# Norms, transposes and operand splits rank 80 earlier in the order of work, and a half's modulation is divided evenly between VectorE and ScalarE

## The chip, the core and the metric

The kernel runs on one core of a Trainium2 chip. The metric is the device time of one execution in microseconds (us). Inputs and outputs are f32 in HBM; nothing of the input is reordered on the way in beyond packed weight arrays, which the kernel streams in their order of use.

The engines, by the names of the profile: PE is TensorE (matmuls and transposes; PEld its weight loads), DVE is VectorE, ACT is ScalarE, POOL is GpSimd, SP is SyncE, which here only issues transfers (DMA).

## The reference

Two models run one after the other on 256 tokens of width 1024, with f32 accuracy. The first has two layers: layer 0 mixes with sliding-window attention and a gated delta rule, layer 1 with a gated recurrence, and each is followed by a squared-ReLU MLP of width 4096. The second has two layers over two streams, the tokens and a context of 256; its mixer joins latent attention (MLA), a 31-tap convolution and a short convolution, and is followed by the same kind of MLP. Cut to what matters:

```python
# first model, both layers
x = layer_norm(DN_ALPHA * x + mix, ln1_g[layer], ln1_b[layer])
x = layer_norm(DN_ALPHA * x + sqrelu_mlp(x, mlp_w1[layer], mlp_w2[layer]), ln2_g[layer], ln2_b[layer])

# second model
def modulation(cvec, w_mod, b_mod):
    m = jax.nn.silu(cvec) @ w_mod + b_mod
    return jnp.split(m[:, None, :], N_MOD, axis=-1)

def modulate(h, shift, scale):
    return h * (1.0 + scale) + shift

def rmsnorm(u, g):
    y = u * lax.rsqrt(jnp.mean(u * u, axis=-1, keepdims=True) + EPS)
    return y * g
```

Each layer of the second model takes `modulate(rmsnorm(x))` into its mixer and into its MLP, and adds `gate * rmsnorm(output)` back to `x`. A layer's six modulation rows come from a matrix of 1024 x 6144.

## The kernel before

**Tiling.** Tokens lie on the 128 partitions: `xt0` and `xt1` are the two token tiles of the main stream, `xc0` and `xc1` those of the context, 128 x 1024 each. A matmul with weights needs its activations transposed, channels on partitions, and to keep f32 accuracy every operand is split in two f32r parts: a high part, the cast of the value, and a low part, value minus high part. A product is three matmuls, high by high, high by low and low by high (`wh`, `wl` are the weights' parts; tiles named `b` hold activations' parts). Weights come in units of 128 x 2048 (`wr`, two buffers) and are split by halves of 1024 (`w_split`, L393 to L409): ScalarE casts the high part (L407), VectorE subtracts for the low part (L408), four buffers each.

**The steps that the change touches.** `to_xT` (L628) turns a token tile's half (512 channels) into operands: four transposes on TensorE into one PSUM bank (`pb` for the first half, `pc` for the second; L366), and then one of two ends. Without modulation, `split` (L454, L455): ScalarE casts, VectorE subtracts. With modulation, 28 halves of the second model: four chunks of 128 x 128 get scale and shift, three on VectorE (L645), one on ScalarE (L647), into one tile `y`; ScalarE casts `y` to the high part (L648), VectorE subtracts (L649). `ln_post` (L654) is the layer norm of the first model. `normed` (L1398) is the second model's norm before a modulation: two sums of squares on ScalarE (L1389), one small VectorE instruction (L1394), the power -1/2 on GpSimd (L1395) and two VectorE scalings (L1408). `post_norm` (L1411) runs `add_normed`: the same sums, two VectorE products with the gate row (L1421, L1423), GpSimd's power (L1395) and two VectorE instructions that add to the stream (L1426).

**What sets the order.** The code is written once, in a straight line, and a scheduler orders each engine's instructions by a rank that counts up as the code is read. `tc.high_priority(n)` sets the rank back by n for what is written under it, so it comes n places earlier than the code says, as far as dependences and buffers allow. Engines run their lists strictly in order: an instruction that waits holds back all behind it. Before the change `post_norm` has 5; the layer-norm chain, `normed` and `to_xT` have none; weight splits have `WS.ahead`; matmuls that fill (`pm`, below) have -10.

**Filling.** The modulation rows are computed by 384 matmuls into tiles `pm` (weights `wm`, `mods()`), which are sprinkled between the others wherever the code calls `fill`.

**Buffers.** Tiles are named by pool: `s2` and `s4` are scratch tiles of 512 and 1024, `ti` the tiny ones, `row` the broadcast rows (3 buffers), `pa` the PSUM banks in which products are summed.

Of the kernel before, what the change touches and what calls it, by code (L numbers as in the profile page):

```python
# [15 lines left out]
P = 128  # L16
BIG = 1.0e30
SM = 1.0 / math.sqrt(96.0)
NW = 4
LEAD = 96  # L20
TRAIL = 24
ALPHA = 4.0 ** 0.25
# [271 lines left out]
def hybrid_then_mla(ctx: ExitStack, tc: tile.TileContext, a, out, usizes):  # L294
# [22 lines left out]
    def s2(shape, dt=F32):  # L317
        return tmp.tile(shape, dt, tag="s2", bufs=9, name=nm("s2"))
# [25 lines left out]
    def v3(ap, n):  # L344
        return ap.rearrange("p (a b) -> p a b", a=n)
# [19 lines left out]
    def tr(o, i):  # L365
        T.transpose(o, i, ident)  # L366
# [86 lines left out]
    def split(ps, h, l):  # L453
        S.copy(h, ps)  # L454
        V.tensor_tensor(l, ps, f(h), op=SUB)  # L455
# [172 lines left out]
    def to_xT(src, t, xT, hfs=(0, 1), off=0, bank=None, mod=None):  # L628


        for hf in hfs:
            ps = (bank or (psB, psC)[hf])()
            for c in range(4):
                o = 512 * hf + 128 * c - off
                tr(ps[:, 128 * c : 128 * c + 128], src[:, o : o + 128])
            sl = (slice(None), slice(4 * hf, 4 * hf + 4), slice(128 * t, 128 * t + 128))
            if mod is None:
                split(v3(ps, 4), xT[0][sl], xT[1][sl])
                continue
            i, st, kind = mod  # L640
            y = s2([P, 4, 128])
            for c in range(4):
                A, B = mcol(i, st, kind, hf, c), mcol(i, st, kind - 1, hf, c)
                if c < 3:
                    V.tensor_scalar(y[:, c, :], ps[:, 128 * c : 128 * c + 128], A, B, op0=MUL, op1=ADD)  # L645
                else:
                    S.activation(y[:, c, :], ps[:, 128 * c : 128 * c + 128], AF.Identity, bias=B, scale=A)  # L647
            S.copy(xT[0][sl], y)  # L648
            V.tensor_tensor(xT[1][sl], y, f(xT[0][sl]), op=SUB)  # L649

    def new_xT():
        return (b8([P, 8, 256], F32R), b8([P, 8, 256], F32R))

    def ln_post(t, halves, g, b, late):  # L654

        x = xt[t]
        st = ti(12, "st", 4)
        for c in range(2):
            cs = slice(512 * c, 512 * c + 512)
            V.scalar_tensor_tensor(x[:, cs], x[:, cs], ALPHA, halves[c], op0=MUL, op1=ADD)  # L660
            V.bn_stats(st[:, 6 * c : 6 * c + 6], x[:, cs])
        mv = ti(2)
        V.bn_aggr(mv, st)
        rs = ti(1)
        rsqrt(rs, mv[:, 1:2], 1, 1.0, 1e-5)
        both = slice(0, 512), slice(512, 1024)
        for cs in both:
            V.scalar_tensor_tensor(x[:, cs], x[:, cs], mv[:, 0:1], g[:, cs], op0=SUB, op1=MUL)
        for cs in both:
            V.scalar_tensor_tensor(x[:, cs], x[:, cs], rs, b[:, cs], op0=MUL, op1=ADD)  # L670
        if late is not None:
            late.fn[t] = lambda: to_xT(x, t, late.xT)

    def softplus(o, x, n):

# [68 lines left out]
    def mcol(i, st, kind, hf, c):  # L744

        o = 8 * c + 4 * (kind % 2) + 2 * hf + (1 - st)
        return mc[:, i, kind // 2, o : o + 1]
# [649 lines left out]

    def normed(x):  # L1398

        ss = ti(2)  # L1400
        y = s4([P, 1024])
        for c in range(2):
            cs = slice(512 * c, 512 * c + 512)
            sumsq(ss[:, c : c + 1], x[:, cs], y[:, cs], 1.0 / 32.0)
        r = rms(ss)
        for c in range(2):
            cs = slice(512 * c, 512 * c + 512)
            V.tensor_scalar(y[:, cs], x[:, cs], r, None, op0=MUL)  # L1408
        return y

    def post_norm(x, halves, GP):  # L1411

        with tc.high_priority(5):
            add_normed(x, halves, GP)

    def add_normed(x, halves, GP):
# [650 lines left out]
```

## Time and profile before

| | |
|---|---|
| median of 3 runs | 1632.86 us (1632.76 to 1634.14) |
| the profiled execution | 1635.88 us, of which the span is 1633.8 us and 2.1 us lie around it |
| PE busy | 1578.0 us, 97% of the span |
| DVE busy | 1029.0 us, 63% |
| ACT busy | 743.3 us, 45% |
| POOL busy | 94.8 us, 6% |
| mean granted clock of TensorE | 0.991 of full speed |

How to read it: PE is busy nearly all the time, so the time that can be had or lost lies in its idle stretches, about 56 us in all, and in stretches in which its clock is at half speed. The view of waits of an engine says what ended its idle time, the timeline shows single instructions with their start, duration and the idle time before them, and the table of stretches gives each engine's busy time and the granted clock between two times. Times on a timeline are us from the start of the span. An instruction's duration can be longer than its distance to the next one on the same engine, because one's end overlaps the next one's start.

### The profile page before, as it was taken

What the parts mean: (1) busy time and instruction counts of PE and PEld (TensorE: products, weight loads), DVE (VectorE), ACT (ScalarE), POOL (GpSimd) and SP (SyncE); (2) the same over time, 40 slices, a digit from 0 to 9 for tenths busy, and PEclk for the clock granted to TensorE, in tenths of its full rate; (3) what the DMA queues carried; (4) which work ended last, traced back from release to release, by engine and by line L of the source; (5) the groups of instructions that cost most, each with busy time, mean ns of one, the idle gap of its engine ahead of it and who ended that gap; (6) DMA issues with size and microseconds to landing.
All of it is one profiled execution on the core that took longest, in us unless ns stands there. A gap on an engine that the chain in (4) does not pass through costs nothing.

```text
span 1633.8 us, 24905 instructions
## 1 busy us (share of the span) xinstructions
PE 1578.0 (97%) x10182; PEld 1358.9 (83%) x10182; DVE 1029.0 (63%) x1593; ACT 743.3 (45%) x1264; POOL 94.8 (6%) x121
## 2 busy tenths in 40 slices
PE   7999999999999999999999999999999999989998
PEld 7866679888878998877877789999999788779997
DVE  6874575556787556768974753444444789775555
ACT  5642244443574445436454543222222475554443
POOL 0021000000000000003010100000000030000000
PEclk9999999999999999999999999999999999989999
DMA  7865475555665554562310432222232262235553
GB/s 289 288 217 172 167 258 196 204 207 191 248 258 181 194 192 169 181 227 80 130 52 27 138 134 89 93 103 85 97 104 79 100 216 107 73 126 201 181 186 124
DMA packets 46946, 259.77 MB, mean 159 GB/s; under 512 B 5600, under 2 KB 5856, under 8 KB 24304
## 3 DMA queue, kind: packets, MB, share of 16 engines
q1 hardware_dynamic: 46832, 258.18, 44.9%
q8 instruction: 80, 1.31, 0.3%
q14 instruction: 34, 0.28, 0.1%
HBM read 257.08 MB, written 1.08 MB: 158 GB/s over the span
## 4 chain that ended last, share of the span: by engine, by line
PE 78%; DVE 8%; ACT 4%; DMA 2%; POOL 1%; issue 1%; POOLq 0%; DVEq 0%; ACTq 0%; SPq 0%
PE pa L342 44%; PE pb L342 27%; PE pm L342 4%; PE pb L366 2%; DVE wl L408 1%; DMA wr<-in_wp_dram 1%; PE pc L366 1%; ACT s L1389 1%; ACT wh L407 1%; DVE s L1583 1%; POOL ti L1395 1%; ACT s L1652 0%; DVE s L645 0%; DVE b L711 0%; DVE xt L1426 0%
## 5 line engine op out<-in xcount | busy, mean ns | idle before, releaser
L408 DVE TENSOR_TENSOR wl<-wr,wh 128x1024 fp32r<-128x1024 f32 (+2 forms) x366 | 443.4, 1217 | 301.4 <-ACT wh L407 288.4
L407 ACT CAST wh<-wr 128x1024 fp32r<-128x1024 f32 (+2 forms) x364 | 376.1, 1041 | 405.8 <-PE pa L342 202.6
L342 PE MATMUL pa<-wh,b 128*128 128x512 f32 (+3 forms) x1456 | 411.1, 365 | 12.5 <-ACT b L816 5.7
L342 PE MATMUL pb<-b,wh 128*128 128x256 f32 x2240 | 406.2, 284 | 0.0
L342 PEld LDWEIGHTS pb<-b,wh 128*128 128x128 f32 x2240 | 352.7, 192 | 7.2 <-issue 3.4
L342 PE MATMUL pb<-b,wl 128*128 128x256 f32 x1120 | 317.8, 284 | 0.0
L342 PEld LDWEIGHTS pa<-wh,b 128*128 128x128 f32 x1456 | 267.6, 195 | 57.1 <-ACT b L648 6.1
L342 PE MATMUL pa<-wl,b 128*128 128x512 f32 (+3 forms) x728 | 258.7, 364 | 8.9 <-DVE wl L408 8.9
L342 PE MATMUL pa<-wh,s 128*128 128x512 f32 x768 | 244.5, 391 | 0.0
L342 PEld LDWEIGHTS pb<-b,wl 128*128 128x128 f32 x1120 | 215.1, 192 | 1.7 <-issue 1.7
L342 PE MATMUL pa<-b,wh 128*128 128x256 f32 x1056 | 199.2, 289 | 3.7 <-ACT wh L407 1.9
L342 PEld LDWEIGHTS pa<-b,wh 128*128 128x128 f32 x1056 | 166.2, 193 | 16.0 <-issue 4.4
L342 PEld LDWEIGHTS pa<-wl,b 128*128 128x128 f32 x728 | 142.3, 195 | 35.3 <-DVE wl L408 13.5
L342 PEld LDWEIGHTS pa<-wh,s 128*128 128x128 f32 x768 | 144.4, 188 | 28.9
L342 PE MATMUL pa<-b,wl 128*128 128x256 f32 x528 | 150.1, 288 | 1.3 <-DVE wl L408 1.3
L342 PE MATMUL pa<-wl,s 128*128 128x512 f32 x384 | 150.4, 392 | 0.0
L342 PEld LDWEIGHTS pa<-b,wl 128*128 128x128 f32 x528 | 101.6, 193 | 8.2 <-DVE wl L408 3.3
L560 DVE TENSOR_TENSOR s<-s 128x512 f32<-128x512 f32 x80 | 54.9, 687 | 50.2 <-ACT s L558 50.2
L342 PE MATMUL pm<-wm,cs_t 128*32 128x512 f32 x384 | 83.2, 606 | 1.9 <-DMA wm<-in_wm_dram 1.7
L342 PEld LDWEIGHTS pa<-wl,s 128*128 128x128 f32 x384 | 72.3, 188 | 14.5 <-DVE wl L408 1.2
L1583 DVE SCALAR_TENSOR_TENSOR s<-cu,cols_sb,s 128x512 f32<-128x512 f32 (+1 forms) x120 | 70.7, 621 | 0.5
L366 PE MATMUL pb<-kc_sb,s 128*128 128x128 f32 x366 | 56.8, 279 | 10.8 <-DVE s L1408 2.5
(278 smaller groups left out, 1391.6 us busy)
## 6 DMA issues: line engine op xcount, KB each, us to landing
wr<-in_wp_dram SPq DMA_DIRECT2D x176, 1024.0 KB, 4.8
wm<-in_wm_dram SPq DMA_DIRECT2D x96, 512.0 KB, 5.2
row<-in_rows_dram SPq DMA_DIRECT2D x10, 512.0 KB, 5.5
wr<-in_wp_dram SPq DMA_DIRECT2D x4, 832.0 KB
s<-in_bg_dram SPq DMA_DIRECT2D x24, 128.0 KB, 5.6
row<-mdr SPq DMA_DIRECT2D x6, 512.0 KB, 3.5
wr<-in_wp_dram SPq DMA_DIRECT2D x4, 264.0 KB, 3.6
b<-in_xT_dram SPq DMA_DIRECT2D x4, 256.0 KB, 6.1
```

What stands on the lines that cost most here:

```text
L342: T.matmul(o, l, r, start=start, stop=stop)
L366: T.transpose(o, i, ident)
L407: S.copy(h[:, :n], r)
L408: V.tensor_tensor(l[:, :n], r, f(h[:, :n]), op=SUB)
L560: V.tensor_tensor(q, r, r, op=MUL)
L1389: S.activation(j, x, AF.Square, scale=scale, accum_out=o)
L1395: G.tensor_tensor(r, e, half[:, :1], op=POW)
L1583: V.scalar_tensor_tensor(ac, src, w(k), ac, op0=MUL, op1=ADD)
```

## The change

`to_xT`, the layer-norm chain (now a function `ln_chain`), `normed` (its body now `rms_normed`) and `post_norm` run under `tc.high_priority(CHAIN)` with `CHAIN = 80`; `post_norm` had 5. In a modulated half the chunks 0 and 1 are VectorE's and 2 and 3 ScalarE's, where VectorE had three; and the high part is cast by VectorE (`V.tensor_copy`) and not by ScalarE.

```diff
+CHAIN = 80
@@ def to_xT(src, t, xT, hfs=(0, 1), off=0, bank=None, mod=None):
-        for hf in hfs:
...
-            for c in range(4):
-                A, B = mcol(i, st, kind, hf, c), mcol(i, st, kind - 1, hf, c)
-                if c < 3:
...
-            S.copy(xT[0][sl], y)
-            V.tensor_tensor(xT[1][sl], y, f(xT[0][sl]), op=SUB)
+        with tc.high_priority(CHAIN):
+            for hf in hfs:
+                ps = (bank or (psB, psC)[hf])()
+                for c in range(4):
+                    o = 512 * hf + 128 * c - off
+                    tr(ps[:, 128 * c : 128 * c + 128], src[:, o : o + 128])
+                sl = (slice(None), slice(4 * hf, 4 * hf + 4), slice(128 * t, 128 * t + 128))
+                if mod is None:
+                    split(v3(ps, 4), xT[0][sl], xT[1][sl])
+                    continue
+                i, st, kind = mod
+                y = s2([P, 4, 128])
+                for c in range(4):
+                    A, B = mcol(i, st, kind, hf, c), mcol(i, st, kind - 1, hf, c)
+                    if c < 2:
+                        V.tensor_scalar(y[:, c, :], ps[:, 128 * c : 128 * c + 128], A, B, op0=MUL, op1=ADD)
+                    else:
+                        S.activation(y[:, c, :], ps[:, 128 * c : 128 * c + 128], AF.Identity, bias=B, scale=A)
+                V.tensor_copy(xT[0][sl], y)
+                V.tensor_tensor(xT[1][sl], y, f(xT[0][sl]), op=SUB)
@@ def ln_post(t, halves, g, b, late):
-        x = xt[t]
+        with tc.high_priority(CHAIN):
+            ln_chain(xt[t], halves, g, b)
+        if late is not None:
+            late.fn[t] = lambda: to_xT(xt[t], t, late.xT)
+
+    def ln_chain(x, halves, g, b):
@@ def normed(x):
+        with tc.high_priority(CHAIN):
+            return rms_normed(x)
+
+    def rms_normed(x):
@@ def post_norm(x, halves, GP):
-        with tc.high_priority(5):
+        with tc.high_priority(CHAIN):
```

The counts of instructions stay the same on every engine but for the 28 halves: ScalarE has 28 casts fewer and 28 chunks more, VectorE 28 chunks fewer and 28 casts more. GpSimd's order stays the same. Of SP's transfers, three weight units (`wr96`, `wr102`, `wr110`) are issued two to five places later and two pairs of `wm` earlier.

The lines of the kernel after are numbered a few higher: L408 is L409, L645 is L647, the cast (L648 before) is L650, L649 is L651, L1394 is L1399, L1408 is L1417, L1421, L1423 and L1426 are L1430, L1432 and L1435.

The first place is TensorE around the second layer's MLP input, at 1433 to 1441 us of the trace before. `pa_1512` is the last bank of the mixer's output product for a token tile, `pb_1523` and `pc_1525` are the transposes of the normed tile `xt0`, `pa_1540` the head of the next product. Before:

```order
L342 MATMUL pa_1512_13426<-wl300_13502,b8_1471_13267 128x512
L342 MATMUL pa_1512_13426<-wh300_13501,b8_1472_13268 128x512
L342 MATMUL pa_1512_13426<-wh301_13507,b8_1471_13267 128x512
L342 MATMUL pa_1512_13426<-wl301_13508,b8_1471_13267 128x512
L342 MATMUL pa_1512_13426<-wh301_13507,b8_1472_13268 128x512
L366 MATMUL pb_1523_13587<-kc_sb_76,s4_1520_13554 128x128 x4
L366 MATMUL pc_1525_13599<-kc_sb_76,s4_1520_13554 128x128 x4
L342 MATMUL pa_1540_13659<-wh302_13511,b8_1507_13421 128x256
```

After:

```order
L343 MATMUL pa_1512_13426<-wl300_13502,b8_1471_13267 128x512
L367 MATMUL pb_1523_13587<-kc_sb_76,s4_1520_13554 128x128 x4
L367 MATMUL pc_1525_13599<-kc_sb_76,s4_1520_13554 128x128 x4
L343 MATMUL pa_1512_13426<-wh300_13501,b8_1472_13268 128x512
L343 MATMUL pa_1512_13426<-wh301_13507,b8_1471_13267 128x512
L343 MATMUL pa_1512_13426<-wl301_13508,b8_1471_13267 128x512
L343 MATMUL pa_1512_13426<-wh301_13507,b8_1472_13268 128x512
L343 MATMUL pa_1540_13659<-wh302_13511,b8_1507_13421 128x256
```

The eight transposes stand ahead of the last four matmuls of `pa_1512` and not behind them.

The second is VectorE at the same place, 1434 to 1442 us. `wl302` to `wl305` are low parts of weights, `s2_1524` and `s2_1526` the two modulated halves of `xt0`, `b8_1507` and `b8_1508` their high and low parts; `s2_1528`, `s2_1529` and `ti_1531` belong to the post-norm of the other token tile, `xt1`. Before:

```order
L408 TENSOR_TENSOR wl302_13512<-wr152_13505,wh302_13511 128x1024
L408 TENSOR_TENSOR wl303_13640<-wr152_13505,wh303_13639 128x1024
L645 TENSOR_SCALAR s2_1524_13592<-pb_1523_13587,mc_96 128x128 x3
L645 TENSOR_SCALAR s2_1526_13604<-pc_1525_13599,mc_96 128x128 x3
L1421 TENSOR_TENSOR s2_1528_13612<-pa_1511_13425,row_1506_13419 128x512
L1394 SCALAR_TENSOR_TENSOR ti_1531_13618<-ti_1527_13611 128x1
L1423 TENSOR_TENSOR s2_1529_13613<-pa_1512_13426,row_1506_13419 128x512
L649 TENSOR_TENSOR b8_1508_13422<-s2_1524_13592,b8_1507_13421 128x4x128
L649 TENSOR_TENSOR b8_1508_13422<-s2_1526_13604,b8_1507_13421 128x4x128
L1426 SCALAR_TENSOR_TENSOR xt1_90<-s2_1528_13612,ti_1532_13619,xt1_90 128x512
L1426 SCALAR_TENSOR_TENSOR xt1_90<-s2_1529_13613,ti_1532_13619,xt1_90 128x512
```

After:

```order
L409 TENSOR_TENSOR wl302_13512<-wr152_13505,wh302_13511 128x1024
L647 TENSOR_SCALAR s2_1524_13592<-pb_1523_13587,mc_96 128x128 x2
L647 TENSOR_SCALAR s2_1526_13604<-pc_1525_13599,mc_96 128x128 x2
L409 TENSOR_TENSOR wl303_13640<-wr152_13505,wh303_13639 128x1024
L1430 TENSOR_TENSOR s2_1528_13612<-pa_1511_13425,row_1506_13419 128x512
L1399 SCALAR_TENSOR_TENSOR ti_1531_13618<-ti_1527_13611 128x1
L1432 TENSOR_TENSOR s2_1529_13613<-pa_1512_13426,row_1506_13419 128x512
L1435 SCALAR_TENSOR_TENSOR xt1_90<-s2_1528_13612,ti_1532_13619,xt1_90 128x512
L1435 SCALAR_TENSOR_TENSOR xt1_90<-s2_1529_13613,ti_1532_13619,xt1_90 128x512
L650 CAST b8_1507_13421<-s2_1524_13592 128x4x128
L650 CAST b8_1507_13421<-s2_1526_13604 128x4x128
L651 TENSOR_TENSOR b8_1508_13422<-s2_1524_13592,b8_1507_13421 128x4x128
```

The whole post-norm of `xt1` stands ahead of the two casts that make the high parts of `xt0`, and `wl303` behind the modulation's chunks.

The third is VectorE in the first layer, at 921 to 930 us, where a context tile's post-norm (`xc0`), the modulation of `xt1` (`s2_1016`, `s2_1018`) and two weight splits meet. Before:

```order
L408 TENSOR_TENSOR wl213_8598<-wr107_8591,wh213_8597 128x1024
L645 TENSOR_SCALAR s2_1016_8785<-pb_1015_8780,mc_96 128x128 x3
L645 TENSOR_SCALAR s2_1018_8797<-pc_1017_8792,mc_96 128x128 x3
L1421 TENSOR_TENSOR s2_1020_8805<-s4_958_8419,row_982_8607 128x512
L1394 SCALAR_TENSOR_TENSOR ti_1023_8811<-ti_1019_8804 128x1
L1423 TENSOR_TENSOR s2_1021_8806<-s4_958_8419,row_982_8607 128x512
L649 TENSOR_TENSOR b8_978_8602<-s2_1016_8785,b8_977_8601 128x4x128
L1426 SCALAR_TENSOR_TENSOR xc0_4721<-s2_1020_8805,ti_1024_8812,xc0_4721 128x512
L649 TENSOR_TENSOR b8_978_8602<-s2_1018_8797,b8_977_8601 128x4x128
L1426 SCALAR_TENSOR_TENSOR xc0_4721<-s2_1021_8806,ti_1024_8812,xc0_4721 128x512
L408 TENSOR_TENSOR wl214_8930<-wr107_8591,wh214_8929 128x1024
```

After:

```order
L647 TENSOR_SCALAR s2_1016_8785<-pb_1015_8780,mc_96 128x128 x2
L647 TENSOR_SCALAR s2_1018_8797<-pc_1017_8792,mc_96 128x128
L1430 TENSOR_TENSOR s2_1020_8805<-s4_958_8419,row_982_8607 128x512
L1432 TENSOR_TENSOR s2_1021_8806<-s4_958_8419,row_982_8607 128x512
L647 TENSOR_SCALAR s2_1018_8797<-pc_1017_8792,mc_96 128x128
L409 TENSOR_TENSOR wl213_8598<-wr107_8591,wh213_8597 128x1024
L1399 SCALAR_TENSOR_TENSOR ti_1023_8811<-ti_1019_8804 128x1
L650 CAST b8_977_8601<-s2_1016_8785 128x4x128
L1435 SCALAR_TENSOR_TENSOR xc0_4721<-s2_1020_8805,ti_1024_8812,xc0_4721 128x512
L1435 SCALAR_TENSOR_TENSOR xc0_4721<-s2_1021_8806,ti_1024_8812,xc0_4721 128x512
L651 TENSOR_TENSOR b8_978_8602<-s2_1016_8785,b8_977_8601 128x4x128
L650 CAST b8_977_8601<-s2_1018_8797 128x4x128
```

`wl214` follows next. Ahead of it stand four chunks of the modulation where there were six, one low part where there were two, and two casts.

## Rows read from the trace of the kernel before

**Rows 1.** The page: busy time of PE, its share, instructions.

```profile
PE 1578.0 (97%) x10182; PEld 1358.9 (83%) x10182; DVE 1029.0 (63%) x1593; ACT 743.3 (45%) x1264; POOL 94.8 (6%) x121
```

**Rows 2.** Waits of PE: line, releaser and its line; us total, times, longest.

```profile
PE pa L342 <- DVE wl L408: 10.2, 8, 2.4
PE pa L342 <- ACT b L648: 7.0, 4, 4.1
...
PE pb L366 <- DVE s L1408: 2.5, 3, 1.1
...
PE pc L366 <- ACT s L647: 2.1, 2, 1.9
PE pc L366 <- DVE s L1725: 2.0, 4, 1.2
...
PE pa L342 <- ACT b L454: 0.8, 2, 0.6
```

**Rows 3.** Groups by line and shape: count, busy us, mean ns; idle before, releaser.

```profile
L648 ACT CAST b<-s 128x512 fp32r<-128x512 f32 x28 | 17.3, 618 | 0.5
L645 DVE TENSOR_SCALAR s<-pb,mc 128x128 f32<-128x128 f32 x42 | 15.0, 404 | 7.0 <-PE pb L366 7.0
...
L1408 DVE TENSOR_SCALAR s<-xt,ti 128x512 f32<-128x512 f32 x16 | 7.1, 484 | 4.2 <-POOL ti L1395 4.1
...
L647 ACT ACTIVATE s<-pb,mc 128x128 f32<-128x128 f32 x14 | 6.4, 456 | 18.5 <-DVE s L645 18.4
...
L405 DVE CAST wh<-wr 128x1024 fp32r<-128x1024 f32 x2 | 1.4, 688 | 0.0
```

**Rows 4.** Stretches: from:to, length, busy of PE, PEld, DVE, ACT, POOL; clock, DMA.

```profile
690.00:780.00 90.00, 84.18 (x550) 69.13 (x548) 68.47 (x126) 47.89 (x97) 17.06 (x24) 0.98 0.41 148
...
1280.00:1345.00 65.00, 60.24 (x388) 50.47 (x387) 56.18 (x124) 40.85 (x92) 15.21 (x25) 1.00 0.44 148
```

**Rows 5.** PE timeline, 205 to 208 us and 753: start, duration, line, instruction.

```profile
205.56 1.05 PE L342 MATMUL pm<-wm,cs_t 128*32 128x512 f32 x2
206.53 0.39 PE L342 MATMUL pa<-wh,b 128*128 128x256 f32 x1
206.85 1.05 PE L342 MATMUL pm<-wm,cs_t 128*32 128x512 f32 x4
207.83 0.38 PE L342 MATMUL pa<-wl,b 128*128 128x256 f32 x1
...
752.93 1.92 PE L342 MATMUL pm<-wm,cs_t 128*32 128x512 f32 x2
```

**Rows 6.** DVE timeline, 921 to 931 us: the split of `wl214`.

```profile
928.82 1.22 DVE L408 TENSOR_TENSOR wl<-wr,wh 128x1024 fp32r<-128x1024 f32 x1
```

**Rows 7.** PE timeline, two heads: idle time and its releaser in brackets.

```profile
930.09 0.58 PE L342 MATMUL pa<-wl,b 128*128 128x256 f32 x1 [2.22 <-DVE wl L408]
...
1439.28 0.58 PE L342 MATMUL pa<-wh,b 128*128 128x256 f32 x1 [4.14 <-ACT b L648]
```

**Rows 8.** DVE timeline, 1434 to 1442 us.

```profile
1434.28 2.35 DVE L408 TENSOR_TENSOR wl<-wr,wh 128x1024 fp32r<-128x1024 f32 x2
1436.54 1.04 DVE L645 TENSOR_SCALAR s<-pb,mc 128x128 f32<-128x128 f32 x3
...
1439.72 1.28 DVE L649 TENSOR_TENSOR b<-s,b 128x512 fp32r<-128x512 f32 x2
1440.92 0.75 DVE L1426 SCALAR_TENSOR_TENSOR xt<-s,ti,xt 128x512 f32<-128x512 f32 x1
```

**Rows 9.** PE by stretches of 3.4 us: length, busy; granted clock, DMA share, GB/s.

```profile
1438.40:1441.80 3.40, 2.52 (x12) 0.50 0.63 265
...
929.80:933.20 3.40, 3.11 (x14) 0.50 0.59 188
```

**Rows 10.** POOL timeline: start, duration of the power of a norm.

```profile
646.38 0.55 POOL L1395 TENSOR_TENSOR ti<-ti,half 128x1 f32<-128x1 f32 x1 [135.36 <-DVE ti L1394]
...
930.25 1.40 POOL L1395 TENSOR_TENSOR ti<-ti,half 128x1 f32<-128x1 f32 x1 [3.47 <-DVE ti L1394]
```

More of the change, by code (lines that the diff above doesn't have):

```diff
@@ L628, in to_xT @@
     def to_xT(src, t, xT, hfs=(0, 1), off=0, bank=None, mod=None):
-        for hf in hfs:
-            ps = (bank or (psB, psC)[hf])()
-            for c in range(4):
[L634 to L642, printed above, removed]
-                A, B = mcol(i, st, kind, hf, c), mcol(i, st, kind - 1, hf, c)
-                if c < 3:
-                    V.tensor_scalar(y[:, c, :], ps[:, 128 * c : 128 * c + 128], A, B, op0=MUL, op1=ADD)
-                else:
-                    S.activation(y[:, c, :], ps[:, 128 * c : 128 * c + 128], AF.Identity, bias=B, scale=A)
-            S.copy(xT[0][sl], y)
-            V.tensor_tensor(xT[1][sl], y, f(xT[0][sl]), op=SUB)
+        with tc.high_priority(CHAIN):
[18 more added lines that the diff above has]
+                V.tensor_tensor(xT[1][sl], y, f(xT[0][sl]), op=SUB)
     def new_xT():
@@ L670, in ln_post @@
             V.scalar_tensor_tensor(x[:, cs], x[:, cs], rs, b[:, cs], op0=MUL, op1=ADD)
-        if late is not None:
-            late.fn[t] = lambda: to_xT(x, t, late.xT)
     def softplus(o, x, n):
```

## The prediction

> **What bounds the kernel now.** I read the page first. PE is busy for 97% of the span [rows 1], so whatever DVE and ACT save counts only where PE stands idle, some 56 us. The view of PE's waits comes next, since it tells who ends that idle time. Few of its entries touch the change: heads of products that wait for the high part of a modulated half, 7.0 us in four waits, the longest 4.1; transposes that wait for `normed`'s scalings, 2.5, for ScalarE's chunk of a modulation, 2.1 (a buffer: `pc` can't be written until its last reader is done), and for the branch norms, 2.0; and a plain operand split, 0.8 [rows 2]. That makes 14.4 us at most. The largest entry, 10.2 us for weights' low parts, belongs to no raised step [rows 2]; DVE's own list decides there. Last I read the granted clock by stretches: after long waits PE runs a stretch of 3.4 us at half speed, 0.50 at 1438.4 and 929.8 [rows 9]. In such a stretch half of the work of 3.4 us is lost, 1.7 us. So a wait has a second price, and one that is shortened may give back more than itself.
>
> **The modulation itself.** Before, a half's path behind its transposes is three DVE chunks, one ACT chunk, the ACT cast. A DVE chunk alone takes 0.40, and three take 1.04, so one more adds 0.32 [rows 3, 8]; the ACT chunk 0.46, the cast 0.62 [rows 3]. Sum 1.04 + 0.46 + 0.62 = 2.1. After: two DVE chunks 0.72, two ACT chunks 0.46 + about 0.40, then a DVE cast. The trace has no DVE cast of 512 elements. The nearest are a DVE cast of 1024 at 0.69, half of which is 0.34, and a DVE scaling of 512 from SBUF at 0.48 [rows 3]; a subtraction of that size at 0.64, two in 1.28 [rows 8], is the upper bound, since it reads a second tensor. I take 0.42, between the first two. The path is then 2.0: a gain of 0.1, which one more crossing between engines can eat. In busy time DVE gets 28 x (0.42 - 0.32) = +2.8 us, ACT loses 28 x (0.62 - 0.40) = 6.2. Neither is the bound, so I cost the new division itself at nothing on the path: PE's other products cover it in most places. Without that cover, at the four heads of rows 2, it is 4 x (-0.1) on one end (cast 0.34: 4 x -0.2) and 4 x (+0.1) on the other (cast 0.64). What counts is on whose list the cast now stands.
>
> **The new order, place by place.** I followed both orders against the starts of the trace, wherever they differ next to a wait or a fill.
>
> *Fills.* `pm` matmuls cost PE by interruptions: two in a row take 0.97 until the next product starts, four take 0.98 [rows 5]. At 203 to 219 us and at 400 to 421 the raised transposes stand further forward, and two interruptions join to one: -0.98 each, less 0.2 and 0.4 for a change of shape that stays. Sum **-1.4**.
>
> *Plain splits.* The L454 wait near 505 us, the larger of two that make 0.8, hides behind the products left: **-0.4**; the wait for weights behind it stays. At 838 to 866 the branch norms' splits and transposes come earlier: a quarter of the 2.0 us [rows 2], **-0.5**.
>
> *Norm of the first second-model tile, 640 to 665.* The raised transposes stand ahead of the last products and wait for L1408 instead of being covered by them: **+0.4**, a part of that row's 2.5 us.
>
> *690 to 780.* PE is idle for 5.8 us there [rows 4]. The first head of the mixer comes later, since a DVE cast queues behind other work: +0.9. One `pm` interruption moves from the half-speed stretch near 752, where it took 1.92, to full speed, 0.97 [rows 5]: -1.0. One more disappears: -1.0. Sum **-1.1**.
>
> *895 to 955.* DVE starts `wl214`, which ends a PE wait of 2.22 us at 930.09, at 928.82 [rows 6, 7]. From `wl213` on, the order drops two chunks, 0.64, and one low part, 0.64, ahead of it and adds two casts, 0.84; it also fills a wait of DVE there, and the chain starts earlier. `wl214` moves forward by about 1.0, and 0.2 is given back at transposes waiting longer for L1408: **-0.8**.
>
> *1280 to 1345.* The order takes away a wait of 1.9 for ACT's chunk [rows 2] and puts transposes behind the last product where they wait 1.1 and 1.15 for L1408; a weight split comes late as well, 1.3 idle, and a later wait of 0.9 and part of another go: **-0.1** of an idle 4.8 [rows 4].
>
> *1426 to 1455.* The transposes now wait for L1408 ahead of four products, which then run 0.9 later. On DVE `wl302` starts at 1434.28; two splits take 2.26 [rows 8], so one ends at 1435.4. Four chunks, 1.3: 1436.7. `wl303`, 1.13: 1437.8. Then the other tile's post-norm: two products, 1.3, with its small instruction, to 1439.2; GpSimd's power, 0.55 when undisturbed [rows 10], ends about then. Two L1426 at 0.7: 1440.7. Only now the cast of `xt0`, 0.42, and a hand-off: 1441.2. Before, PE's head started at 1439.28 [rows 7]: +2.0. PE runs at half speed until 1445.2, which the delay partly covers with idle time, so about +1.0 is left there; the next head, near 1451, starts some 2.2 later, less the half-speed stretch that may leave. Ends +0.5 and +4.2; I take **+1.8**, as the first head's delay is certain by the order and the second's is half covered.
>
> *The rest.* At the end of the kernel (post-norms, 1611 on) the orders agree. Three weight units are issued later by up to five transfers; the buffers' readers, not the transfers, set their splits, so nothing, or up to +1 if the cover of one is gone.
>
> **Sum:** -1.4 - 0.4 - 0.5 + 0.4 - 1.1 - 0.8 - 0.1 + 1.8 = -2.1 us against the profiled execution's 1635.88 (its span and 2.1 us around it), 1633.8. That execution lies 3.0 us above the median of 1632.86; the difference is carried over to the median: 1630.8, rounded to **1631**. A measurement of this kernel can tell about 0.2%, 3.3 us, from no change, so this is no change that can be told.
>
> **The rivals.**
>
> *Casts behind chains (slower).* ACT's cast had a list of its own to stand on; DVE's cast ranks equal with the raised post-norm of another tile and stands behind its power step. The order shows it at 1439, at its twin near 1451 and near 925 and 1300, where `xc` tiles' post-norms meet modulated halves. If three of these heads come 2.0 later than my terms say, as the first does at 1439, that is +6: **1637**. For it: DVE is busy for 56 of 65 us in one of these stretches [rows 4]. Against: in the first-layer place the list ahead of the products gets shorter. It decides from the point at which PE's waits for the cast exceed the 7.0 us they had for L648 by 3 or more.
>
> *The clock comes back (faster).* If the shorter wait at 930, the absent fill near 752 and a displaced wait near 1451 keep PE's clock up, up to three half-speed stretches of 1.7 each go: two of them -3.4, and with them the sum is -5.5, **1627**. For it: the fall at 929.8 comes with the 2.2 wait that I expect to halve [rows 7, 9], and the wait of 1.9 for ACT's chunk near 1296 was followed by none, the clock being 1.00 all through its stretch [rows 2, 4]. Against: near 752 and 1451 the order leaves most of the waits ahead of the stretch as they are.
>
> *GpSimd held up by casts.* The power step takes 0.55 with DVE quiet and 1.40 when it starts under a weight split [rows 10], so some DVE instructions block it. If the casts do, each of some eight power steps on a path would lose a cast's 0.42: +3.4, **1634**. The trace shows no DVE cast under a power step. The Trainium skill ("SBUF — State Buffer", section "Who interferes with whom") says that a VectorE cast may enter a mode with two ports and then holds the ports it shares with GpSimd to its end, which speaks against the change; it says the same of an instruction with two SBUF inputs, and there the 1.40 agrees.
>
> *Nothing moves.* Where PE waits, it's the same weights; gains and losses of a few tenths cancel: **1633**.
>
> **How the numbers follow.** My sum 0.35, casts behind chains 0.20, the clock 0.25, GpSimd 0.10, nothing 0.10. Faster than 1629.6: the clock's 0.25 and a fifth of my sum's, 0.32. Slower than 1636.1: three quarters of the first rival's, 0.15, and 0.05 for GpSimd's losses on top of late heads, 0.20. Within: 0.48. The range reaches below the clock's 1627 by one more stretch, to 1625, and above the slow case's 1637 by 1, to 1638.
>
> **What would show it.** In the profile after: the cast's mean (0.34 to 0.48) on DVE; PE's waits for it beside the 7.0 of L648; the head at 1439 later by 2 against its surroundings; the wait for `wl214` near 1 us; the number of half-speed stretches (such as those at 929.8 and 1438.4 [rows 9]); the power step's mean. Wrong would be the sum if PE's waits for L1408 grew by more than 3 us, as raised transposes waiting in line would do, or if stretches at half speed appeared at new places.

## The result: slower by 0.65%

The changed kernel takes 1642.82 us in the median of four runs (1641.44 to 1648.11), the kernel before 1633.06 beside it: a ratio of 1.0065, 95% interval 1.0041 to 1.0088. Run again later it took 1641.73 us against 1634.36, 1.0044 (1.0030 to 1.0058). The forecast was 1631, no change that can be told. The profiled execution of the changed kernel took 1648.11 us, its span 1646.1.

The page of the changed kernel, busy time by engine, answers to [rows 1]:

```profile
span 1646.1 us, 24907 instructions
PE 1584.5 (96%) x10182; PEld 1359.5 (83%) x10182; DVE 1030.2 (63%) x1593; ACT 738.1 (45%) x1264; POOL 90.8 (6%) x121
```

DVE and ACT moved the way reckoned (+2.8 and -6.2), by +1.2 and -5.2 us, and it did not matter. PE's idle time grew from 56 to 62 us. Its busy time grew by 6.5 with the same instructions: the same work lasts longer at half speed, but not all of it is that, and in a second trace of the changed kernel (number 12) it is only 2.9 more than before. The waits of PE, for [rows 2]:

```profile
PE pa L343 <- DVE wl L409: 8.7, 8, 2.9
PE pa L343 <- DVE b L650: 6.7, 2, 5.1
PE pb L367 <- DVE s L1417: 6.1, 10, 1.1
...
PE pm L343 <- DMA wm<-in_wm_dram: 3.0, 2, 2.8
PE pa L343 <- ACT s L1661: 2.6, 2, 2.1
PE pc L367 <- DVE s L1734: 2.4, 4, 1.7
```

The waits for a modulated half's high part (L650) went from four to two, but the longest from 4.1 to 5.1. Waits for `normed`'s scalings (L1417) went from 2.5 us in three to 6.1 in ten: the raised transposes queue on PE's list for them. The groups of the steps that changed, mean ns of one behind the busy time:

```profile
L1400 POOL TENSOR_TENSOR ti<-ti,half 128x1 f32<-128x1 f32 x26 | 17.3, 667 | 770.0 <-DVE ti L1399 770.0
L650 DVE CAST b<-s 128x512 fp32r<-128x512 f32 x28 | 11.7, 422 | 2.6 <-ACT s L649 2.5
```

PE by stretches of 3.3 to 3.4 us, with the granted clock behind the count, for [rows 9]:

```profile
704.10:707.40 3.30, 3.30 (x9) 0.50 1.02 340
...
864.50:867.80 3.30, 3.30 (x13) 0.50 0.00 1
933.50:936.90 3.40, 3.14 (x25) 1.00 0.75 224
1407.20:1410.60 3.40, 3.40 (x18) 0.50 0.00 0
1448.20:1451.60 3.40, 2.46 (x10) 0.50 0.38 161
1451.60:1454.90 3.30, 3.30 (x17) 0.50 0.07 10
1461.90:1465.20 3.30, 2.68 (x12) 0.50 0.00 0
1465.20:1468.60 3.40, 3.40 (x18) 0.50 0.00 0
```

The stretch at 930 (here 933) is back at full speed. New ones stand at 704, 864 and 1407, and the one at 1452 (here 1462) is twice as long.

**Where the time went.** I paired each PE instruction of one trace with its namesake in the trace of before and took how much later it starts, place by place. The first column is the working of the prediction, the others are differences in us between the two ends of a place (times of before), for both traces of the changed kernel and for runs below:

```
place       forecast  after  again | order  divis.  post5  noNormed   g1     g2     g3   layer0  best
190-235        -0.8   -0.64  -0.92 | -0.95   0.61  -0.90   -0.92   -0.52  -0.95   0.03   0.81  -0.98
395-445        -0.6   -0.45  -0.47 | -0.43   0.00  -0.37   -0.46   -0.48  -0.53  -0.44  -0.01  -0.57
640-668         0.4    0.13   0.13 |  0.15   0.16   0.14    0.17    0.13   0.15   0.14   0.00   0.01
688-735 \      -1.1    3.45   2.97 |  4.71   0.93   2.93   -1.84   -1.81   3.00  -1.83   1.17  -0.21
735-785 /             -0.07  -0.09 | -0.09   0.03  -0.09    0.02    0.06  -0.06   0.04   0.03  -0.10
838-872        -0.5    1.43   1.27 |  0.51   0.00   2.78    1.41    0.51   0.51   1.44   0.00   0.92
885-955        -0.8   -0.50  -0.51 |  1.11  -3.88  -2.40   -2.37   -0.50  -0.49  -0.51  -3.89  -3.88
1270-1380      -0.1    1.36   1.38 |  4.23   5.24   3.68    4.00    1.42   2.19   1.37   0.83  -0.42
1380-1415       0      2.17   3.02 |  1.59   1.27   0.00   -0.98    3.06   3.03   2.17   0.01   0.02
1426-1448 \     1.8    3.37   2.91 |  0.42   0.53  -0.17    3.07    2.49  -0.81  -0.26   0.03  -0.25
1448-1465 /            1.33   1.09 | -0.11   0.25   0.23    1.13    0.25   1.42   0.39   0.00  -0.01
```

(Left out are the start to 190 us and 445 to 520 us, where half-speed stretches come and go between traces, also between two with the same order, before and number 8. The forecast of -0.4 at 488 to 520 is not seen, 0.00: the wait for the plain split fell from 0.8 to 0.2, but the one for weights behind it grew from 2.4 to 2.9.) In the two traces of the changed kernel the places agree within 0.9 us, most within 0.3, so most of what an order does to a place repeats. Not all of it does. Up to 913 us every engine's list in number 8 is that of the kernel before, and yet its trace loses 0.8 at 190 to 235 and 1.2 at 688 to 735, where it has a half-speed stretch and before has none. A difference of about 1 us at one place of one trace can thus be the execution's own. Two places carry the larger part of the loss, 688 to 735 and 1426 to 1465, and three more add to it.

The first. PE's timeline of the changed kernel, fill matmuls and waits at 697 to 707 us:

```profile
697.73 1.92 PE L343 MATMUL pm<-wm,cs_t 128*32 128x512 f32 x14
702.41 1.05 PE L343 MATMUL pm<-wm,cs_t 128*32 128x512 f32 x4 [2.76 <-DMA wm<-in_wm_dram]
703.69 3.16 PE L343 MATMUL pm<-wm,cs_t 128*32 128x512 f32 x6 [0.22 <-DMA wm<-in_wm_dram]
```

The same place before:

```profile
698.08 1.92 PE L342 MATMUL pm<-wm,cs_t 128*32 128x512 f32 x14
700.27 0.66 PE L366 MATMUL pc<-kc_sb,s 128*128 128x128 f32 x4 [0.27 <-ACT s L647]
702.60 2.25 PE L342 MATMUL pm<-wm,cs_t 128*32 128x512 f32 x8 [1.67 <-DMA wm<-in_wm_dram]
```

Before, the row of 14 was followed by four transposes, then a row of 8 behind a wait of 1.67. Now 24 stand in one row. The `wm` buffers of the last ten are filled only when the first ones are read (issued from 698.81 on, 3.6 to 4.5 us to landing), and PE has nothing else on its list: one piece of 2.8 us, and the clock falls at 704.

The second. DVE and then PE of the changed kernel at 1444 to 1449 us, for [rows 7, 8]:

```profile
1444.26 1.22 DVE L409 TENSOR_TENSOR wl<-wr,wh 128x1024 fp32r<-128x1024 f32 x1
1445.39 0.69 DVE L1430 TENSOR_TENSOR s<-pa,row 128x512 f32<-128x512 f32 x1
1445.99 0.16 DVE L1399 SCALAR_TENSOR_TENSOR ti<-ti 128x1 f32<-128x1 f32 x1
1446.06 0.69 DVE L1432 TENSOR_TENSOR s<-pa,row 128x512 f32<-128x512 f32 x1
1446.88 1.41 DVE L1435 SCALAR_TENSOR_TENSOR xt<-s,ti,xt 128x512 f32<-128x512 f32 x2
1448.21 0.76 DVE L650 CAST b<-s 128x512 fp32r<-128x512 f32 x2
...
1448.68 0.58 PE L343 MATMUL pa<-wh,b 128*128 128x256 f32 x1 [5.05 <-DVE b L650]
```

The casts stand behind the whole post-norm of the other tile, and PE's head starts right after the first of them.

### The profile page after: what moved, and what is told of

It reads as the page before. It is cut to its first block, busy times and chain, and to the rows that moved or that the text cites. A ratio compares the mean times of both kernels' runs of the same rounds, so it can differ in the third digit from the quotient of the medians.

```text
span 1646.1 us, 24907 instructions
## 1 busy us (share of the span) xinstructions
PE 1584.5 (96%) x10182; PEld 1359.5 (83%) x10182; DVE 1030.2 (63%) x1593; ACT 738.1 (45%) x1264; POOL 90.8 (6%) x121
## 4 chain that ended last, share of the span: by engine, by line
PE 78%; DVE 9%; ACT 4%; POOL 2%; issue 2%; DMA 1%; POOLq 0%; DVEq 0%; ACTq 0%; SPq 0%
PE pa L343 44%; PE pb L343 27%; PE pm L343 3%; PE pb L367 2%; DVE wl L409 1%; PE pc L367 1%; POOL ti L1400 1%; DVE s L1592 1%; ACT s L1394 1%; DMA wr<-in_wp_dram 1%; DVE s L647 0%; ACT wh L408 0%; DVE b L716 0%; DVE s L1417 0%; DVE xt L1435 0%
## 5 line engine op out<-in xcount | busy, mean ns | idle before, releaser
L409 DVE TENSOR_TENSOR wl<-wr,wh 128x1024 fp32r<-128x1024 f32 (+2 forms) x366 | 442.9, 1216 | 302.2 <-ACT wh L408 295.9
L408 ACT CAST wh<-wr 128x1024 fp32r<-128x1024 f32 (+2 forms) x364 | 376.2, 1042 | 405.8 <-PE pa L343 195.9
```

The costliest lines, as they stand in the source:

```text
L408: S.copy(h[:, :n], r)
L409: V.tensor_tensor(l[:, :n], r, f(h[:, :n]), op=SUB)
```

## The experiments

Ratios are against the kernel before, run beside on the same chip, with 95% intervals. "Raised" is by 80.

**1. The order alone**, and **2. the division alone.** Each undoes the other half of the change:

```diff
# order alone              # division alone
-  if c < 2:               -  with tc.high_priority(CHAIN):   (to_xT, ln_post, normed)
+  if c < 3:               +  if True:
-  V.tensor_copy(...)      -  with tc.high_priority(CHAIN):   (post_norm)
+  S.copy(...)             +  with tc.high_priority(5):
```

> Undoes one part of the change: the four steps rank 80 earlier as in the changed kernel, but a half's modulation is three chunks on VectorE, one on ScalarE, and ScalarE casts the high part, as before. Theory A (the raised order costs the time): as slow as the changed kernel, 1641 to 1645 us, with the wait for the wm transfer near 702 us at 2.8 us and the wait of the first head near 1440 us at about 5 us. Rival B (the cast on VectorE's list costs it): 1631 to 1635, the head near 1440 waiting about 4 us as before. Rival C (both are needed, since the raised post-norm only delays a cast that stands on VectorE's list): 1632 to 1637, with the 702 us wait as in the changed kernel but the head near 1440 not later than before.

> Does one part alone: the even division of a half's modulation with the cast on VectorE, and every rank as before (post_norm 5, nothing else raised). Theory A (order): 1631 to 1635. Rival B (the cast on VectorE): 1639 to 1645, with PE's waits for the cast above the 7.0 us of before. Rival C (both needed): 1631 to 1636.

Order alone: 1644.33 us, 1.0063 (1.0048 to 1.0078). Division alone: 1637.02, 1.0014 (1.0004 to 1.0024). So the order costs the time, theory A, and it does so with one half-speed stretch of 3.4 us fewer than before (four against five between 520 us and the end); but the two don't add place by place. At 1426 to 1448 neither loses much alone (0.42 and 0.53 in the table), together 3.4: rival C holds there. The head's wait there was 3.4 with the order alone, not the 5 that theory A expected. At 885 to 955 the division alone gains 3.9, and the order takes it away.

**3. post_norm back at 5**, and **4. to_xT not raised**, both from the changed kernel:

```diff
# 3                                      # 4
-  with tc.high_priority(CHAIN):         -  with tc.high_priority(CHAIN):
+  with tc.high_priority(5):             +  if True:
       add_normed(x, halves, GP)              for hf in hfs:
```

> The changed kernel with post_norm's rank back at 5; all else raised. If the late heads near 1440 and 1451 us come from the raised post-norm chain that stands ahead of the casts on VectorE, the first of the two starts 1.5 to 2 us earlier against its surroundings (a wait of 3.5 to 4 us and not 5.1), PE's waits for the cast fall from 6.7 to 5 us or less, and the time is 1637 to 1640. If they come from something else (the transposes ahead of the last products), nothing moves: 1641 to 1645.

> The changed kernel with to_xT (transposes, splits, modulation) not raised; norms and post-norms raised by 80. If the raised transposes cost the time by standing ahead of products and waiting for normed's scalings, PE's waits for those scalings fall from the 6.4 us of the changed kernel towards the 2.5 us of before and the time is 1634 to 1638. If the norms and post-norms are what costs, 1640 to 1645.

The third took 1637.97 us, 1.0025 (1.0015 to 1.0035): more than half of the loss gone, PE's waits for L650 at 3.9 with a longest of 2.2, and 1426 to 1448 back at -0.17. The fourth took 1649.72 us, 1.0094 (1.0079 to 1.0110), slower than either expectation. PE's waits for the scalings fell as expected, from 6.1 to 4.0, but those for L650 rose from 6.7 in two to 10.1 in five, the longest from 5.1 to 7.1. That transposes which are not raised come later still when norms and post-norms are is my reading; no run tests it.

**5. post_norm raised alone**, from the kernel before (`tc.high_priority(80)` in place of 5):

> The kernel before with one number changed: post_norm ranks 80 earlier and not 5. Nothing else is raised, the modulation is as before. Putting post_norm back took the changed kernel from about 10.6 us over before to about 4.1. If that 6.5 us is post_norm's own price (its chains push other work of VectorE and ScalarE back), this kernel is 4 to 8 us slower than before. If it is a joint price with the cast on VectorE's list, which then stands behind the chain, this kernel is within 2 us of before, and the head near 1440 us starts as before.

1637.56 us, 1.0013 (1.0002 to 1.0023): 2 us, not 6.5. The price of raised post-norms is mostly a joint one.

**6. Chunks alone** (`if c < 2`, cast on ScalarE), and **7. cast alone** (`V.tensor_copy`, three chunks and one), from the kernel before:

> The kernel before with chunks two and two, the cast still on ScalarE, no rank changed. The whole division alone cost 2.3 us. If the chunk does it: 1 to 3 us slower than before. If the cast does it: within 1 us of before.

> The kernel before with the cast on VectorE, chunks three and one as before, no rank changed. If the cast's place on VectorE's list costs the 2.3 us of the division: 2 to 4 us slower than before, since VectorE gets the whole 0.4 us more per half. If the chunk does it: within 1 us.

Chunks: 1633.82 us, 0.9995 (0.9985 to 1.0006). Cast: 1638.93, 1.0025 (1.0014 to 1.0035). The cast on DVE's list is what the division costs; its largest loss is 3.9 us at 1300 to 1350, in the second layer's mixer. PE waits for no cast there. What is new at 1270 to 1380 are waits for `wm`, 1.2 us (1.5 with the whole division), where before has none.

**8. The division ahead of the first layer's MLP only**, no rank changed:

```diff
+  ev = i == 0 and kind == 4
-  if c < 3:
+  if c < (2 if ev else 3):
-  S.copy(xT[0][sl], y)
+  (V.tensor_copy if ev else S.copy)(xT[0][sl], y)
```

> The kernel before with the even division (two chunks each, cast on VectorE) only in the four tiles' modulation ahead of the first layer's MLP (895 to 955 us), no rank changed. With the division alone everywhere that stretch was 3.9 us shorter (2.2 us less idle time, 1.7 from a half-speed stretch that went), while 1300 to 1350 was 4.2 longer. If the places are independent: 2 to 4 us faster than before, 1629 to 1632 beside a before of 1633 to 1634.6, with the wait for wl214 near 930 us gone. If the gain was only the clock's chance: within 1 us of before.

1632.34 us, 0.9988 (0.9976 to 0.9999): the stretch 885 to 955 is 3.9 shorter, as with the division everywhere. PE at 929 to 933 us of this run's trace, in which the head that waited 2.22 for `wl214` waits no more and the clock stays:

```profile
926.60:930.00 3.40, 3.40 (x31) 1.00 0.15 63
929.80:933.20 3.40, 3.21 (x28) 1.00 0.68 224
```

**9. All raised but post_norm, old modulation**, and **10. the changed kernel without normed raised:**

```diff
# 10
 def normed(x):
-    with tc.high_priority(CHAIN):
+    if True:
         return rms_normed(x)
```

> to_xT, the layer-norm chain and normed rank 80 earlier; post_norm stays at 5, and the modulation is the old one (three chunks and one, cast on ScalarE). The order as a whole with the old modulation cost 10 us, post_norm's rank alone 2. If the prices add up: about 8 us slower than before, 1641 to 1644. If raised post-norms and raised norms and transposes cost by meeting each other: 1 to 4 us slower, 1635 to 1638, with the stretch from 905 to 955 us as in the kernel before or shorter.

> The changed kernel with normed not raised; to_xT, the layer-norm chain and post_norm are, and the division is the new one. If normed, which stands behind its own tile's post-norm and takes its sums from ScalarE, is what meets the raised post-norms: 3 us or more faster than the changed kernel, 1638 to 1640. If it is not: within 2 us of the changed kernel, or slower, as the kernel without the raised to_xT was.

Nine: 1637.53 us, 1.0020 (1.0009 to 1.0030), no sum of prices, which would have made 8 us. Ten: 1633.09, 0.9993 (0.9983 to 1.0003): without this one class of calls the loss is gone. Not by what I expected, though: the head near 1440 still waits 5.0 there, and the gain is 5 us at 688 to 735 and 3 to 4 at 1380 to 1415, with 2.6 given back at 1270 to 1380. PE's waits for L1417 are still 5.7 us in ten, so they aren't what the class costs.

**11. The parts that gain:** number 8, with `ln_chain` raised, and `to_xT` raised only in the first model:

```diff
+  with (tc.high_priority(80) if mod is None and bank is None else contextlib.nullcontext()):
```

> The kernel before with the parts that showed a gain: the even division and VectorE's cast only ahead of the first layer's MLP, and to_xT and the layer-norm chain raised by 80 only in the first model, without modulation and without the mixers' own transposes. The stretches 190 to 235 and 395 to 445 were 0.9 and 0.4 us shorter with these raised. If the parts add: 1 to 1.5 us faster than the even division in layer 0 alone, 0.15 to 0.25% faster than before. If fill matmuls fall into worse places behind: no faster than that kernel, or slower than before.

1628.16 us (1627.17 to 1628.87), 0.9960 (0.9946 to 0.9974): faster than both kernels, and by more than its parts. The first model's places are 0.98 and 0.57 shorter than before, as forecast. Against number 8 another 1.4 at 688 to 735 and 1.2 at 1270 to 1380 were not forecast, but the first is mostly number 8's own half-speed stretch, which before lacks with the same lists, and at the second the lists of numbers 8 and 11 are equal; against before they are 0.2 and 0.4.

**12. The changed kernel again:**

> The changed kernel once more, beside the others on one chip, for a second trace. What belongs to the order repeats: the wait for the wm transfer near 702 us (2.8), the head near 1448 waiting about 5 us, more idle time at 1300 to 1380. What is chance of the clock does not: the half-speed stretches near 704, 864 and 1407. Time 1641 to 1646, 0.5 to 0.8% over before.

1641.73 us, 1.0044 (1.0030 to 1.0058). The waits repeat (2.60 for `wm`, 5.0 at the head). So do the places of the half-speed stretches, which I had put down to chance (the one at 1401 is twice as long here); in this trace, all earlier by some 6 us:

```profile
697.80:701.10 3.30, 3.13 (x7) 0.50 1.04 348
858.20:861.50 3.30, 3.16 (x12) 0.50 0.02 7
1400.90:1404.20 3.30, 3.25 (x16) 0.50 0.00 0
```

**13 to 15. One call at a time**, from the changed kernel: one call of `normed` (that of `mlp_block1`, at the passage to the second model) not raised; one call of `post_norm` (second layer's mixer) at 5; both.

```diff
# g1
-                y = normed(xt[t])
+                y = normed(xt[t], False)
# g2
-            post_norm(xs[1][t], halves, GP)
+            post_norm(xs[1][t], halves, GP, 5)
```

> The changed kernel with one call of normed not raised: the two token tiles at the passage from the first model to the second, where the changed kernel runs 24 fill matmuls in one row, waits 2.8 us for a wm transfer and falls to half speed near 704 us. Theory (raised norms there push the modulated transposes behind the fills, so that two short waits become one long one and the clock falls): the row of 24 splits, the stretch 688 to 735 gets 4 to 5 us shorter, and the kernel is 3 to 5 us faster than the changed one, 1637 to 1639. Rival (the wait for the transfer is fixed by the wm buffers and comes back elsewhere): within 1.5 us of the changed kernel.

> The changed kernel with one call of post_norm back at rank 5: that of the second layer's mixer. On VectorE the two casts of xt0 then stand right behind the weight split, ahead of xt1's post-norm; on TensorE only eight transposes move. Theory (the cast stands behind the other tile's post-norm): the first head near 1440 starts 2 to 2.5 us earlier against its surroundings, its wait goes from 5.0 to about 3, the stretch 1426 to 1465 gets 3.5 to 4.5 us shorter, all else repeats, and the kernel is 3 to 4.5 us faster than the changed one, 1637.5 to 1639. Rival (the transposes ahead of the last products are the cause): the head stays, within 1 us of the changed kernel.

> The changed kernel with both of these calls as before. If the two places are independent and carry the loss: 7 to 9 us faster than the changed kernel, 1632.5 to 1635, within 0.2% of before. If the loss sits in the many small places as well: 1636 to 1639.

g1: 1635.95 us, 1.0011 (1.0000 to 1.0023). The stretch 688 to 735 goes from +3.0 to -1.8. Most other places stay as in the changed kernel; 838 to 872 is 0.8 shorter than in its second trace and 1426 to 1465 is 1.3 shorter, with the same lists there and one half-speed stretch fewer in each. PE's fills in this trace:

```profile
691.58 1.06 PE L344 MATMUL pm<-wm,cs_t 128*32 128x512 f32 x8
...
693.01 1.06 PE L344 MATMUL pm<-wm,cs_t 128*32 128x512 f32 x6
...
699.72 1.32 PE L344 MATMUL pm<-wm,cs_t 128*32 128x512 f32 x8
```

Products stand between 694 and 699.7, in which the transfer lands; there is no wait for `wm` at all, and no fall of the clock. PE's idle time in the stretch is 0.3 us, where the changed kernel has 3.0. The rival, a wait fixed by the buffers that comes back elsewhere, falls.

g2: 1639.02 us, 1.0025 (1.0015 to 1.0035). On PE only eight transposes move. PE's head in its trace:

```profile
1441.05 0.41 PE L343 MATMUL pa<-wh,b 128*128 128x256 f32 x1 [2.23 <-DVE b L650]
```

Its wait is 2.2 where it was 5.0, and 1426 to 1465 goes from +4.0 to +0.6. The transposes ahead of the last products stayed where the change put them, so they aren't the cause; the cast behind the chain is.

g3: 1634.84 us, 1.0004 (0.9995 to 1.0013). Putting two calls back is enough to undo the loss, within what can be measured. It isn't the whole account: in this trace 838 to 872, 1270 to 1380 and 1380 to 1415 still lose 5.0 us, and gains at 395 to 445, 688 to 735 and 885 to 955 make up for 2.8 of them. Nor is it the only way, since number 10 gets there with the head near 1440 still late.

**16. to_xT raised everywhere**, the layer-norm chain raised, the division as in number 8, `normed` and `post_norm` as before:

> The kernel before with to_xT raised everywhere, the layer-norm chain raised, normed and post_norm as before, and the even division in layer 0's MLP alone. Beside the best kernel so far it raises the modulated transposes and the mixers' own as well. If raised transposes are harmless by themselves: 1627 to 1630, as that kernel. If they give waits to TensorE's list by themselves (transposes that wait for normed ahead of products): 1631 to 1635.

1633.89 us, 0.9995 (0.9985 to 1.0006): 6 us behind number 11. Raised transposes by themselves cost in the second model; 1270 to 1350 is 4.8 longer in this trace. PE is idle there for 0.8 less than before (1270 to 1380). What grew is the number of fill rows: 48 `pm` matmuls stand in 12 rows in place of 7, and the rows take 11.8 us up to the next product in place of 8.6. Raising can split fills as well as join them.

## Why the prediction was wrong

**What held.** The new cast takes 0.42 us, as taken. The head at 1440 was worked out at 1441.2 for the first start; in the trace it starts at 1448.68, of which 7.56 us are the lag of the products just ahead, by the same pairing: 1441.1. The `wl214` wait, forecast at 1.0, is 0.75 and its half-speed stretch left. The first model's two places came out at -1.1 and -1.4 for -1.4, where rows of two and four fills did join to one of six. The gain at 885 to 955 came within 0.3, but partly by luck: the clock's return there, which the sum left out, was offset by eight more fills that now run in this place (24 for 16; 4.0 us up to the next product for 2.8).

**690 to 780 (forecast -1.1, measured +2.9 to +3.4): the step that failed.** I counted `pm` interruptions: one fewer, -1.0, one moved out of the half-speed stretch near 752, -1.0, and took each at 0.97 whatever its length [rows 5]. The count was off: 64 fills stand in eight rows between 688 and 785 in both traces, and a row of eight, 1.87, took the moved one's place at half speed. So was the price. In the trace before, rows of two, six and eight take 0.98, 0.99 and 1.00 up to the next product, but the row of ten at 402 takes 1.83, so joining 14 and 8 saves no interruption. The +0.9 for the mixer's head didn't come; between 685 and 735 PE waits for `wm` alone. Most of all, what the interruption waits for was left out. In [rows 5] the `wm` tiles lie ready; the joined row of 24 reads tiles whose loads start only when the row's first tiles are free. Products between the fills hide that load; joined fills wait for it. g1 takes the row apart by one call of `normed` and turns +3.0 into -1.8. A part of that, about 1 us, is the clock's, which also fell there in numbers 5 and 8 with the lists of before (+1.8 and +1.2). In number 8, PE's wait and then its stretch:

```profile
699.38 3.17 PE L344 MATMUL pm<-wm,cs_t 128*32 128x512 f32 x8 [1.73 <-DMA wm<-in_wm_dram]
...
699.50:702.90 3.40, 3.40 (x10) 0.51 1.04 425
```

**1426 to 1465 (+1.8 against +4.0 to +4.7): the right mechanism, mis-sized.** The first head came as worked out. The term failed in what I set against it: that half-speed time would cover half of the delay, and that the stretch of the second head might leave. It doubled (two of 3.4 us in place of one). PE's idle time in the place grew by 3.1 us in each of the two traces; the rest goes with the one more stretch at half speed. g2 and the first rival, casts behind chains, agree on the cause. But the rival expected three such heads, and there was one with its twin; its test, PE's waits for the cast above 10 us, would have missed it, since these were 6.7: two other such waits had gone.

**The clock, in one direction only.** I weighed half-speed stretches as something that could go (the rival at 1627) and named new ones only as what would make me wrong, with no price in the sum. One went, at 930. New ones came at 704, 864 and 1407, and the second head near 1450 got one more. PE's longest wait grew at each of the first three, 1.67 to 2.76, 1.20 to 1.66, 1.36 to 2.08, while the idle time of 1380 to 1415 even fell by 0.3. The 18 traces bear out at three places that the stretch goes with the longest wait. At 688 to 712 it stands in the ten with 1.73 to 2.77 and in none of the eight others, with 0.16 to 1.67. At 1380 to 1415 it stands in the eleven with 1.80 to 2.08 and in none with 0.46 to 1.37; at 885 to 955 in the two with 2.22 and 2.58 and in none with up to 1.28. At 838 to 872 the wait doesn't tell: of ten traces with the same waits there, the longest 1.65 to 1.66, five have the stretch, and number 11 has it with 1.20. Number 14, for one, waits as long as the changed kernel and stays at full speed:

```profile
858.75 0.66 PE L367 MATMUL pc<-kc_sb,s 128*128 128x128 f32 x4 [1.66 <-DVE s L1734]
...
857.20:860.60 3.40, 1.84 (x12) 1.00 0.37 133
```

The price of 1.7 us was too high as well. Where traces have the same lists and waits, a fall costs 0.8 to 0.9 at 838 to 872 (1.27 to 1.44 against 0.49 to 0.51), a second stretch at 1380 to 1415 costs 0.9 (3.03 to 3.06 against 2.17), and the fall of number 8 at 688 to 735 costs 1.2. Four came and one went, which makes some 3 us net, an estimate from these, about a third of the loss. The larger part is idle time and rows of fills.

**838 to 872 (-0.5 against +1.3 to +1.4).** I took a quarter of the waits for L1725 off. They rose, 2.0 to 2.4. In the runs in which `to_xT` isn't raised (2, 4 to 8) this place is at 0.00 or 0.01. Raised there, it loses 0.5 in the five traces without a half-speed stretch; the rest of the +1.3 to +1.4 is the clock. A sign error, which I put down to transposes ahead of work that others wait for; that isn't tested by itself.

**The division, costed at nothing.** As a total that is not far off, +2.3 us alone. As a reading of places it is wrong: 3.9 shorter at 885 to 955, 5.2 longer at 1270 to 1380. I said that other products cover the cast, and at 1270 to 1380 they do: PE waits for none. What is new there are waits of fills for their transfers (number 7). That the cast brings them by pushing back what stands behind it on DVE's list is likely, but not tested.

**GpSimd held up by casts** falls by its size. The power step took 0.67 in the mean, where it had 0.88: the raised order moved it out from under weight splits (six of the 26 began under one before, one does now). Four power steps of the changed kernel meet a cast; two of them, POOL and DVE in turn:

```profile
704.28 0.65 POOL L1400 TENSOR_TENSOR ti<-ti,half 128x1 f32<-128x1 f32 x1 [4.19 <-DVE ti L1399]
...
704.10 0.43 DVE L650 CAST b<-s 128x512 fp32r<-128x512 f32 x1
...
1304.69 0.55 POOL L1400 TENSOR_TENSOR ti<-ti,half 128x1 f32<-128x1 f32 x1 [8.65 <-DVE ti L1399]
...
1304.73 0.43 DVE L650 CAST b<-s 128x512 fp32r<-128x512 f32 x1 [0.19 <-ACT s L649]
```

At 704 a cast had begun 0.18 us earlier, and the step lost 0.10; at 1304 it began 0.04 later, and it lost nothing. The rival priced it at 0.42. The rule of the Trainium skill ("SBUF — State Buffer", section "Who interferes with whom"), that between GpSimd and a VectorE instruction in a two-port mode whoever issues first has the shared ports for the whole instruction, agrees in its sense. The three steps that began under a cast had 0.25, 0.26 and 0.20 us of it left and lost 0.10, 0.11 and 0.05. That the cast was in such a mode no run shows.

**A sign of being wrong that came.** PE's waits for L1417 grew by 3.6 us, more than the 3 that I had named. They aren't the loss, though: number 10 keeps 5.7 us of them and takes the time of before.

**What stays open.** What lengthens PE's longest wait at 1380 to 1415 in eleven of the orders I didn't follow, nor what tips the clock at 838 to 872 between traces with equal waits. The +1.4 at 1270 to 1380 is seen in both traces of the changed kernel and not explained. The price of the clock comes from pairs of traces and not from a run of its own: no kernel here kept PE busy in those waits.

## What to carry to other kernels

Raising a whole class of steps in an in-order schedule moves what stands between others as well: look for work that was apart and is now joined (fills whose transfer needs the products between them) and for an instruction that changed its engine and now stands behind a raised chain. Raise calls one by one, and keep those whose place gains: of the same ideas, three parts gave 0.4%, all of them cost 0.4 to 0.65%. Where the clock can fall, look at the longest wait in one piece and not at the sum of waits, and expect that traces with equal waits can still differ.

## What was not expected of the hardware

Half-speed stretches are partly the program's and partly the execution's. Two traces of one kernel have them at the same places after the first 520 us (704, 864, 1407, 1448 and 1462; 698, 858, 1401, 1442 and 1455, with the same 6 us between), while at the start they vary. But with equal lists they can also come and go later: numbers 13 and 14 lack the one at 864, and numbers 5 and 8 have one near 700 that the kernel before lacks. One trace alone doesn't tell what an order does to the clock. Every kernel here executes the same 10182 PE instructions, and PE's busy time still ranged from 1576.0 us (number 10) to 1584.5 (the changed kernel, 1580.9 in its second trace); the fastest kernel, number 11:

```profile
PE 1577.6 (97%) x10182; PEld 1356.7 (83%) x10182; DVE 1027.5 (63%) x1593; ACT 742.7 (46%) x1264; POOL 95.8 (6%) x121
```
